# Token tiles ahead of the modulation's weights, and the second half of an output projection prepared during the first

## The chip, the cores and the metric

One Trainium2 chip, and of it one core. A core has five engines with instruction streams of their own: TensorE (PE; its weight loads are PEld in the profile), VectorE (DVE), ScalarE (ACT), GpSimd (POOL) and SyncE (SP), and 16 DMA engines that move data between the large memory and the on-chip buffers. In this kernel nearly all transfers are issued by SP, in the order of its stream. The metric is the time of one execution in microseconds on the device, as the median over runs.

## The reference

A trunk of two layers over 1024 tokens of width 1024. Each layer normalises the rows, modulates them with a shift and a scale that come from a conditioning vector c, mixes tokens, projects back and adds the gated result. The first layer's mixer is a gated DeltaNet with 16 value heads of 128, the second a softmax attention with a forget gate.

```python
cond = jax.nn.silu(c)
for i in range(DEPTH):                                  # DEPTH = 2
    mod = cond @ ada_w[i] + ada_b[i]                    # 1024 -> 3 * 1024
    shift, scale, gate = jnp.split(mod[:, None, :], 3, axis=-1)
    h = rmsnorm(x, norm_w[i]) * (1 + scale) + shift
    y = gdn_mixer(h, ...) if i == 0 else fox_mixer(h, ...)
    x = x + gate * y
return rmsnorm(x, final_norm_w)

def gdn_mixer(h, w_in, conv_w, A_log, dt_bias, norm_w, w_out):
    qkv, z, b, a = split(h @ w_in)                      # 1024 -> 6176
    ...                                                 # conv, SiLU, l2 norms, gated delta rule
    o = rmsnorm(o, norm_w) * jax.nn.silu(z)
    return o.reshape(B, S, 2048) @ w_out                # 2048 -> 1024
```

All is float32. The change touches two places of the first layer: the norm and modulation at the very start, and the product with `w_out`.

## The kernel before

Products of full accuracy are made from three fast ones: each operand is split into a rounded part `hi` and a rest `lo`, and `mm3` adds hi·hi, hi·lo and lo·hi. `split` does this: ACT rounds (a cast), DVE or POOL subtracts.

The order of TensorE's instructions is written out by the program: `Flow` keeps a clock of its own and a list of generators with priorities, and lets each emit work when its wait (a yielded number, or `hold` on a condition) is over; `flow.bank` hands out PSUM banks and `flow.free` returns them. The other engines' streams, SP's among them, are ordered by a scheduler from dependences and program order. Buffers are named tiles with a number of copies: a new use of a copy waits until the last reader of its former content is done.

**The start.** `start_norm` (called by `proj_all`) handles the first 512 tokens in four tiles of 128 x 1024 from `x` (512 KB each; in `vtok` and once in a `d` tile): `norm_tile` takes the sum of squares on ACT, scales on DVE, and transposes on TensorE into the banks `tr`; ACT copies the result out. Then `ada_load(0)` and `ada_load(1)` fetch shift and scale columns of `ada_w`, eight tiles of 512 KB each, into tiles that are idle then (`og`, `zg`, `gb`, `vt` and `d`; several tiles of different tags print as `d`). DVE accumulates the first KPE of them (7, then 5) into one tile, and `ada_sum` adds the others and that one over partitions with matmuls into the bank `su`; the result gives `gcol` and `scol` for four of the eight feature blocks, and `modulate(k)` makes `ht_h` and `ht_l` of each block and multiplies it with a small weight (`wbh`, `wbl`) into the bank `pc`. Only then can the projections run (`mm` banks, weights `whi`, `wlo`).

**The output projection.** `out_proj_a` computes 1024 tokens by 2048 inputs by 1024 columns in two halves of 512 tokens (h=0, 1), each in two pairs of token tiles (tp=0, 2). The gated DeltaNet's output stands in DRAM as `og_d` and `ogl_d` (hi and lo), 16 blocks k of 128 features. For h=0 columns go in two strips of 512, a weight tile (512 KB) holds two k, and the rows of a k come by `out_o` into `ohi` and `olo` (128 KB each, four copies). For h=1 all 1024 columns go at once, a weight tile is one k, four PSUM banks are used (`mm` and, from the next stage, `lg`), and the rows come by `out_pair`, two k at a time, into `yh` and `yl` (256 KB each, four copies). These two tiles and the `lg` banks belong to the second stage's pools, which open only when the DeltaNet's are given back.

Weights pass through `wtile`: a raw tile (three copies, in the space of `ht_h`), then `whi` (three copies) and `wlo` (five). `w_src` and `o_src` list loads not yet begun, `wq` and `oq` hold those begun; `wnext(ahead)` keeps `ahead` k in `wq`, `oload(n)` keeps n in `oq`. `out_list(h)` fills the lists of a half; before, `out_list(1)` is called at the top of h=1, after the wait for the second stage's banks. In the trace's names `ht_h<-in_wa_o_dram` is such a weight load, `tg` (a `wlo` tile) takes the evacuation, and `x_d` and `v` are the finished rows written and read again by the second layer's norm.

Of the kernel before, what the change touches and what calls it, by code (L numbers as in the profile page):

```python
# [15 lines left out]
P = 128  # L16
D = 1024
# [3 lines left out]
HALF = 512  # L21
# [57 lines left out]
SC = 1.0  # L79
OGW = 2000  # L80
OL = 4
Y_NN = 8000
KPE = (7, 5)
KC = 3
# [110 lines left out]
def tile_trunk(  # L195
# [173 lines left out]
    wq, w_src, wcache = [], [], {}  # L369
    oq, o_src = [], []  # L370
# [3 lines left out]
    def half(n=1):  # L374
        for _ in range(min(n, len(later))):
            later.pop(0)()

    def wload():
        half(2)
        if w_src:  # L380
            wq.extend(w_src.pop(0)())
            if not w_src or w_src[0].__name__ == "load_out":
                oload(2)

# [3 lines left out]

    def wnext(ahead):
        half(2)  # L390
        while len(wq) < ahead and w_src:
            wload()
        return wq.pop(0)

    def wtile(n):
# [52 lines left out]
    def out_pair(k, tok):  # L448
        def load():
            w = 2 * P  # L450
            pr = []
            for n, d in (("yh", og_d), ("yl", ogl_d)):
                v = where["py"].tile([P, 2, w], F32R, name=n, tag=n, bufs=4)
                nc.sync.dma_start(v.bitcast(F32), d[k : k + 2, :, tok : tok + w].rearrange("k p t -> p k t"))
                pr.append(v)
            return [(pr[0][:, i], pr[1][:, i]) for i in range(2)]

        return load

    def out_list(h):  # L460
        n = (512, D)[h]
        for tp in range(0, CPH, 2):
            for cs in range(0, D, n):
                w_src.extend(out_w(k, cs, n) for k in range(0, 16, D // n))
                if h:
                    o_src.extend(out_pair(k, h * HALF + tp * P) for k in range(0, 16, 2))
                else:
                    o_src.extend(out_o(k, tp * P) for k in range(16))

    def out_proj_a():  # L470
        gx = xt_([P, 4, D], "ht_h")
        gb0 = gx[:, 0]
        where["raw"] = [gx[:, i] for i in range(1, 4)]
        for h in range(2):
            n = (512, 1024)[h]
            if h:
                yield from hold(lambda: "bank" in where)
                yield OGW
                out_list(1)
            xs = xt_([P, CPH, D], "ht_l")  # L480
            for tp in range(0, CPH, 2):
                for cs in range(0, D, n):
                    acc = None
                    for k in range(16):
                        wh, wl = wnext((5, 3)[h])
                        oload((OL, 7)[h])
                        hi, lo = oq.pop(0)
                        if acc is None:
                            acc = []
                            for b in range(2 + 2 * h):  # L490
                                acc.append((yield from (acc_bank if b < 2 else where["bank"])()))
                        if (tp, cs, k) == (0, 0, 2):
                            if h == 0:
                                nc.sync.dma_start(gb0, gate_d[0:1, :].broadcast_to([P, D]))
                            for t in range(CPH):
                                r0 = (h * CPH + t) * P
                                nc.sync.dma_start(xs[:, t], x[r0 : r0 + P, :])
                        for t in range(2):
                            o = slice(t * P, (t + 1) * P)
                            for c in range(n // 512):  # L500
                                wc = slice(c * 512, c * 512 + 512)
                                mm3(acc[2 * c + t], hi[:, o], lo[:, o], wh[:, wc], wl[:, wc], k == 0, k == 15)
                            if h:
                                yield 0
                        if not h:
                            yield 0
                    for t in range(2):
                        for c in range(n // 512):
                            c0 = cs + c * 512
                            tg = xt_([P, D], "wlo", 5)[:, 0:512]  # L510
                            nc.vector.tensor_tensor(tg, acc[2 * c + t], gb0[:, c0 : c0 + 512], op=ALU.mult)
                            flow.free(acc[2 * c + t], R_OA + 600 * (2 * c + t))
                            xv = xs[:, tp + t, c0 : c0 + 512]
                            nc.gpsimd.tensor_tensor(xv, xv, tg, op=ALU.add)
                for t in range(tp, tp + 2):
                    nc.sync.dma_start(x1_d[h * CPH + t], xs[:, t])
                    if h:
                        where["n2read"](h * CPH + t, xs[:, t])
                    xdone[h * CPH + t] = flow.t

    with ExitStack() as sa:
# [36 lines left out]
        def start_norm():  # L558
# [58 lines left out]
                nc.vector.tensor_tensor(scol[0][:, cs], ps[:, 0:4], bcol[:, 0, cs], op=ALU.add)  # L617
                flow.free(ps, R_AD)

            pc = yield from pst("tr", 2)  # L620

            def modulate(k):
                xk = xsT[k]
                sc, sh = gcol[0][:, k : k + 1], scol[0][:, k : k + 1]
# [6 lines left out]
                mm3(pc[0:32], wbh[:, k], wbl[:, k], ht_h[:, k], ht_l[:, k], k == 0, k == KT - 1)  # L631

            ws = ada_load(0)
            split(wbh, wbl, wba, lo_eng=nc.vector)
            yield from ada_sum(0, ws)
            for k in range(4):
# [1298 lines left out]
```

## Time and profile before

| | |
|---|---|
| median of 3 runs | 1959.63 us (1958.54 to 1962.46) |
| the profiled execution | 1963.85 us, span 1962.1 us |
| mean granted TensorE clock | 0.976 |
| busy: PE, PEld, DVE, ACT, POOL | 93%, 78%, 68%, 53%, 19% of the span |
| moved by DMA | 307 MB, mean 157 GB/s |

A row of the timeline gives start, duration, engine, line, operation, the tile written, the tiles read, and the count of instructions that were put together; in brackets stands how long the engine stood idle before it and what ended that. Line numbers are those of the kernel before. A row of the chain gives start, duration and what the end of the program hung on at that time. A row of stretches gives the stretch, its length, the busy time (and count) of PE, PEld, DVE, ACT and POOL, the granted clock, the share of the DMA engines and GB/s. A matmul's own duration (0.39 us) is longer than the step from one to the next (0.23), since they overlap.

### The profile page before, as it was taken

To read this page: it belongs to the slowest core of one execution; us is meant where nothing else is said; L and a number is where in the kernel's file an instruction comes from. 1 tells how busy PE (TensorE), PEld (TensorE's weight loads), DVE (VectorE), ACT (ScalarE), POOL (GpSimd) and SP (SyncE) were. 2 spreads that over 40 slices of the span, in tenths; PEclk is the share of its full clock that TensorE was granted. 3 is DMA by queue.
4 is the path that set the end of the run, shared out by engine and by line. 5 is a ranking of instruction groups with operands and counts; after the bars stand their busy time and mean duration, and the time that the engine had idled before them with its cause. 6 is when DMAs were issued, how large, how long until landed. Compare 5 with 4: busy or idle time off the path is not lost.

```text
span 1962.1 us, 35871 instructions
## 1 busy us (share of the span) xinstructions
PE 1825.4 (93%) x12888; PEld 1522.8 (78%) x12888; DVE 1326.6 (68%) x3323; ACT 1031.5 (53%) x2674; POOL 365.8 (19%) x402
## 2 busy tenths in 40 slices
PE   5989999989999999999898599999999999999798
PEld 4767787777787777888776478788988988889676
DVE  5586988788887678776655386365666656656764
ACT  4465666655654555555444353365556556655631
POOL 1010111111110100110001144223133132231322
PEclk9889999999999999999999799999999999999899
DMA  7475757677666556454589893011011111111422
GB/s 267 162 239 183 237 192 241 217 227 235 225 185 196 175 169 199 149 171 133 184 275 321 320 308 134 18 60 65 18 60 49 44 60 39 49 54 65 157 88 94
DMA packets 224922, 307.16 MB, mean 157 GB/s; under 512 B 100397, under 2 KB 136877, under 8 KB 224745
## 3 DMA queue, kind: packets, MB, share of 16 engines
q1 hardware_dynamic: 223736, 304.65, 47.8%
q8 instruction: 101, 1.65, 0.4%
q14 instruction: 77, 0.62, 0.1%
q10 hardware_dynamic: 1008, 0.23, 0.1%
HBM read 223.15 MB, written 81.67 MB: 155 GB/s over the span
## 4 chain that ended last, share of the span: by engine, by line
PE 68%; DMA 12%; DVE 12%; ACT 4%; issue 2%; SPq 1%; POOL 1%; ACTq 0%; DVEq 0%; POOLq 0%
PE mm L136 42%; PE lg L136 6%; PE su L136 4%; PE pt L140 4%; PE oT L136 3%; PE tr L140 3%; PE ch L136 3%; DMA nx<-in_ada_w_dram 2%; PE co L136 2%; DVE wlo L339 2%; DMA ht_h<-in_wa_o_dram 1%; DMA ohi<-og_d 1%; DMA rmat<-rb 1%; DVE cv_y L824 1%; ACT whi L336 1%
## 5 line engine op out<-in xcount | busy, mean ns | idle before, releaser
L136 PE MATMUL mm<-ht_h,whi 128*128 128x512 f32 x768 | 342.7, 446 | 0.5 <-DVE nh L312 0.5
L136 PE MATMUL mm<-ht_h,wlo 128*128 128x512 f32 x768 | 305.6, 398 | 0.0
L136 PE MATMUL mm<-ht_l,whi 128*128 128x512 f32 x768 | 304.9, 397 | 0.2 <-POOL ht_l L339 0.2
L136 PE MATMUL mm<-whi,h_h 128*128 128x384 f32 x512 | 186.5, 364 | 0.9 <-DVE kn L1524 0.9
L136 PEld LDWEIGHTS mm<-ht_h,wlo 128*128 128x128 f32 x768 | 146.5, 191 | 33.6
L136 PE MATMUL mm<-whi,h_l 128*128 128x384 f32 x512 | 172.5, 337 | 0.0
L136 PE MATMUL mm<-wlo,h_h 128*128 128x384 f32 x512 | 172.4, 337 | 0.0
L136 PEld LDWEIGHTS mm<-ht_h,whi 128*128 128x128 f32 x768 | 147.6, 192 | 28.7 <-issue 2.1
L1675 DVE TENSOR_TENSOR ptl<-pt,pth 128x512 fp32r<-128x512 f32 x192 | 106.3, 555 | 93.1 <-ACT pth L1674 91.4
L136 PEld LDWEIGHTS mm<-ht_l,whi 128*128 128x128 f32 x768 | 147.9, 193 | 24.4 <-POOL ht_l L339 0.6
L1674 ACT CAST pth<-pt 128x512 fp32r<-128x512 f32 x192 | 91.2, 476 | 141.2 <-PE pt L140 140.5
L824 DVE SCALAR_TENSOR_TENSOR cv_y<-cv_t,conv_h,cv_y 128x512 f32<-128x512 f32 x192 | 143.3, 746 | 17.6 <-ACT cv_y L816 15.3
L339 DVE TENSOR_TENSOR wlo<-ht_h,whi 128x512 fp32r<-128x512 f32 x124 | 93.2, 792 | 56.0 <-ACT whi L336 46.7
L1639 ACT ACTIVATE lg<-lg,mx 128x896 f32<-128x896 f32 (+7 forms) x128 | 99.5, 777 | 54.3 <-DVE mx L1631 48.5
L1518 POOL TENSOR_TENSOR rs<-ss,mhalf 128x4 f32<-128x4 f32 x64 | 64.5, 1007 | 331.1 <-DVE ss L1516 328.4
L336 ACT CAST whi<-ht_h 128x512 fp32r<-128x512 f32 x124 | 70.7, 618 | 90.5 <-PE mm L136 38.1
L136 PE MATMUL mm<-h_h,whi 128*128 128x512 f32 x240 | 100.5, 419 | 0.7 <-DVE wlo L1774 0.3
L136 PEld LDWEIGHTS mm<-whi,h_h 128*128 128x128 f32 x512 | 97.5, 190 | 3.5 <-ACT v L1520 1.2
L140 PE MATMUL pt<-ident,lg 128*128 128x128 f32 (+1 forms) x584 | 96.1, 274 | 3.5 <-ACT lg L1639 3.5
L136 PEld LDWEIGHTS mm<-wlo,h_h 128*128 128x128 f32 x512 | 96.9, 189 | 2.0
L136 PEld LDWEIGHTS mm<-whi,h_l 128*128 128x128 f32 x512 | 96.2, 188 | 0.0
L136 PE MATMUL mm<-h_h,wlo 128*128 128x512 f32 x240 | 94.9, 395 | 0.0
(384 smaller groups left out, 4486.5 us busy)
## 6 DMA issues: line engine op xcount, KB each, us to landing
ht_h<-in_wa_o_dram SPq DMA_DIRECT2D x62, 512.0 KB, 5.3
wc<-whi SPq DMA_DIRECT2D x45, 512.0 KB, 4.2
wc<-wlo SPq DMA_DIRECT2D x45, 512.0 KB, 4.2
wlo<-wc SPq DMA_DIRECT2D x45, 512.0 KB, 4.8
whi<-wc SPq DMA_DIRECT2D x45, 512.0 KB, 3.6
wlo<-in_wa_c_dram SPq DMA_DIRECT2D x35, 512.0 KB, 4.7
nx<-in_ada_w_dram SPq DMA_DIRECT2D x64, 256.0 KB, 3.5
wraw<-in_wb_dram SPq DMA_DIRECT2D x56, 256.0 KB, 2.7
```

The source lines that it names most:

```text
L136: self.nc.tensor.matmul(out, lhsT, rhs, start=start, stop=stop)
L140: self.nc.tensor.transpose(out, src, ident)
L336: nc.scalar.copy(hi, src)
L339: (lo_eng or nc.gpsimd).tensor_tensor(lo, src, hi.bitcast(F32), op=ALU.subtract)
L824: nc.vector.scalar_tensor_tensor(y, raw[:, j : j + HALF], w[:, j : j + 1], y, op0=ALU.mult, op1=ALU.add)
L1518: nc.gpsimd.tensor_tensor(rs, ss, mhalf[:, 0:4], op=ALU.pow)
L1639: nc.scalar.activation(lg, lg, AF.Exp, scale=-1.0, bias=mx[:, hh : hh + 1], accum_out=sums[:, tt : tt + 1],)
L1674: nc.scalar.copy(ph_[:, cs], pp[:, cs])
L1675: nc.vector.tensor_tensor(pl_[:, cs], pp[:, cs], ph_[:, cs].bitcast(F32), op=ALU.subtract)
```

## The change

At the start `ada_load(0)` is called before the bank `pc` is taken rather than after it; the token loads keep their place in the program, ahead of both. In the output projection, `out_list(1)` is called during the first half (last strip, k=8) rather than at the top of the second; the first OX=4 blocks k of the second half's first pair use `out_o` (tiles `ohi`, `olo`) in place of `out_pair`; and `wid`, `wno` number the weight tiles in `wq`, so that no more than three of them are in hand at a time.

```diff
+OX = 4
...
+    wid, wno = [], [0]
+
     def wload():
         half(2)
-        if w_src:
-            wq.extend(w_src.pop(0)())
+        if w_src and len(set(wid)) < 3:
+            ws = w_src.pop(0)()
+            wno[0] += 1
+            wid.extend([wno[0]] * len(ws))
+            wq.extend(ws)
             if not w_src or w_src[0].__name__ == "load_out":
                 oload(2)
...
     def wnext(ahead):
         half(2)
-        while len(wq) < ahead and w_src:
+        while len(wq) < ahead and w_src and len(set(wid)) < 3:
             wload()
+        wid.pop(0)
         return wq.pop(0)
...
                 if h:
-                    o_src.extend(out_pair(k, h * HALF + tp * P) for k in range(0, 16, 2))
+                    k0 = 0 if tp else OX
+                    o_src.extend(out_o(k, h * HALF + tp * P) for k in range(k0))
+                    o_src.extend(out_pair(k, h * HALF + tp * P) for k in range(k0, 16, 2))
...
                 yield OGW
-                out_list(1)
...
                         wh, wl = wnext((5, 3)[h])
+                        if not h and (tp, cs, k) == (2, D - n, 8):
+                            out_list(1)
                         oload((OL, 7)[h])
...
-            pc = yield from pst("tr", 2)
-
...
             ws = ada_load(0)
+            pc = yield from pst("tr", 2)
             split(wbh, wbl, wba, lo_eng=nc.vector)
```

The scheduler orders the streams anew. On SP, at the very start, before:

```order
L563 DMA vtok<-in_x_dram 128x1024
L588 DMA og<-in_ada_w_dram 128x2x512
L588 DMA zg<-in_ada_w_dram 128x2x512
L588 DMA d_285<-in_ada_w_dram 128x2x512
L588 DMA og<-in_ada_w_dram 128x2x512
L588 DMA zg<-in_ada_w_dram 128x2x512
L588 DMA gb<-in_ada_w_dram 128x2x512
L588 DMA vt<-in_ada_w_dram 128x2x512
L588 DMA d_300<-in_ada_w_dram 128x2x512
L563 DMA vtok<-in_x_dram 128x1024 x2
L563 DMA d_240<-in_x_dram 128x1024
L414 DMA wlo<-in_wa_c_dram 128x1024
```

and at the same place in the change:

```order
L573 DMA vtok<-in_x_dram 128x1024 x3
L573 DMA d_240<-in_x_dram 128x1024
L598 DMA og<-in_ada_w_dram 128x2x512
L598 DMA zg<-in_ada_w_dram 128x2x512
L598 DMA d_284<-in_ada_w_dram 128x2x512
L598 DMA og<-in_ada_w_dram 128x2x512
L598 DMA zg<-in_ada_w_dram 128x2x512
L598 DMA gb<-in_ada_w_dram 128x2x512
L598 DMA vt<-in_ada_w_dram 128x2x512
L598 DMA d_299<-in_ada_w_dram 128x2x512
L421 DMA wlo<-in_wa_c_dram 128x1024
```

Three of the four token tiles moved from behind the first eight weight tiles to ahead of them. On DVE, around the first `gcol`, before:

```order
L596 SCALAR_TENSOR_TENSOR d_348<-d_355,cond,d_348 128x1024
L596 SCALAR_TENSOR_TENSOR d_348<-og,cond,d_348 128x1024
L596 SCALAR_TENSOR_TENSOR d_348<-zg,cond,d_348 128x1024
L613 TENSOR_TENSOR gcol_88<-su,bcol 128x4
L617 TENSOR_TENSOR scol_90<-su,bcol 128x4
L614 SCALAR_TENSOR_TENSOR gcol_88<-gcol_88,norm_c 128x4
L629 TENSOR_SCALAR k<-k,gcol_88,scol_90 128x512
L630 TENSOR_TENSOR ht_l<-k,ht_h 128x512
L629 TENSOR_SCALAR k<-k,gcol_88,scol_90 128x512
L630 TENSOR_TENSOR ht_l<-k,ht_h 128x512 x2
L339 TENSOR_TENSOR wlo<-wlo,whi 128x512 x2
L630 TENSOR_TENSOR ht_l<-q,ht_h 128x512
```

and in the change (`d_348` is the accumulation of the modulation's second half):

```order
L606 SCALAR_TENSOR_TENSOR d_348<-d_355,cond,d_348 128x1024
L623 TENSOR_TENSOR gcol_88<-su,bcol 128x4
L627 TENSOR_TENSOR scol_90<-su,bcol 128x4
L624 SCALAR_TENSOR_TENSOR gcol_88<-gcol_88,norm_c 128x4
L606 SCALAR_TENSOR_TENSOR d_348<-og,cond,d_348 128x1024
L637 TENSOR_SCALAR k<-k,gcol_88,scol_90 128x512
L606 SCALAR_TENSOR_TENSOR d_348<-zg,cond,d_348 128x1024
L638 TENSOR_TENSOR ht_l<-k,ht_h 128x512
L637 TENSOR_SCALAR k<-k,gcol_88,scol_90 128x512
L638 TENSOR_TENSOR ht_l<-k,ht_h 128x512 x2
L638 TENSOR_TENSOR ht_l<-q,ht_h 128x512
L340 TENSOR_TENSOR wlo<-wlo,whi 128x512 x4
```

Two accumulations moved behind `gcol`, and the splits of a weight tile behind the fourth `ht_l`. On SP, at the end of the first half of the output projection, from the last transfers of DeltaNet's output on, before:

```order
L1133 DMA og_d<-ogh 128x512
L1133 DMA ogl_d<-ogl 128x512
L1133 DMA og_d<-ogh 128x512
L516 DMA x_d<-ht_l 128x1024
L426 DMA ht_h<-in_wa_o_dram 128x1024
L1133 DMA ogl_d<-ogl 128x512
L516 DMA x_d<-ht_l 128x1024
L426 DMA ht_h<-in_wa_o_dram 128x1024 x2
L1363 DMA v<-x_d 128x1024
L342 DMA kn<-in_wb_dram 128x512
```

and in the change:

```order
L1142 DMA og_d<-ogh 128x512
L1142 DMA ogl_d<-ogl 128x512
L450 DMA ohi<-og_d 128x256
L450 DMA olo<-ogl_d 128x256
L450 DMA ohi<-og_d 128x256
L433 DMA ht_h<-in_wa_o_dram 128x1024
L450 DMA olo<-ogl_d 128x256
L450 DMA ohi<-og_d 128x256
L450 DMA olo<-ogl_d 128x256
L433 DMA ht_h<-in_wa_o_dram 128x1024
L450 DMA ohi<-og_d 128x256
L1142 DMA og_d<-ogh 128x512
```

The rows of the second half's k=0 to 3 are new there (the last `olo` of them follows two rows on), and two weight loads moved up. A few rows on, SP's stream up to the first `yh` and `yl`, before:

```order
L1363 DMA v<-x_d 128x1024
L342 DMA kn<-in_wb_dram 128x512
L1363 DMA v<-x_d 128x1024
L342 DMA kn<-in_wb_dram 128x512
L1363 DMA v<-x_d 128x1024
L1418 DMA qk_c<-in_qkn_dram 128x2
L454 DMA yh<-og_d 128x2x256
L1421 DMA fb<-in_f_bias_dram 128x16
L454 DMA yl<-ogl_d 128x2x256
```

and in the change, where the first `yh` holds k=4 and 5:

```order
L433 DMA ht_h<-in_wa_o_dram 128x1024
L1372 DMA v<-x_d 128x1024
L343 DMA kn<-in_wb_dram 128x512
L1372 DMA v<-x_d 128x1024
L433 DMA ht_h<-in_wa_o_dram 128x1024
L343 DMA kn<-in_wb_dram 128x512
L1372 DMA v<-x_d 128x1024
L1427 DMA qk_c<-in_qkn_dram 128x2
L1430 DMA fb<-in_f_bias_dram 128x16
L461 DMA yh<-og_d 128x2x256
L461 DMA yl<-ogl_d 128x2x256
```

Weight loads moved in among the norm's tiles, ahead of the first `yh`. The order of TensorE's instructions is the same in both; only the tiles that 48 matmuls read have other names.

## The prediction

> **What bounds the kernel now.** First the page: TensorE is busy 93% of the span, so only a stretch in which it stands still, or waits for its data, can give time.
>
> ```profile
> PE 1825.4 (93%) x12888; PEld 1522.8 (78%) x12888; DVE 1326.6 (68%) x3323; ACT 1031.5 (53%) x2674; POOL 365.8 (19%) x402
> ```
>
> The profiled execution took 1963.85 us, 1.75 of it outside its span of 1962.1, and lies 4.2 us above the median of the runs (1959.63). I sum against it and carry the difference to the median. The edit touches two such stretches, and I read each by itself: the chain that ended last, then SP's queue, then the transfer rate. The first is the start, before any projection runs:
>
> ```profile
> 10.90 8.12 DMA vtok<-in_x_dram
> ...
> 25.59 1.97 PE tr L140 x8
> 27.57 1.12 PE tr L140 x4
> 28.69 6.63 PE su L136 x32
> ...
> 35.34 0.16 DVE gcol L613
> ...
> 35.80 2.93 ACT ht_h L625 x4
> ```
>
> The chain goes over the token tiles: the sums `su` stand behind the transposes `tr` on TensorE, and the transposes wait for tiles that were asked for behind eight weight tiles:
>
> ```profile
> 10.39 0.47 SPq L588 DMA_DIRECT2D d<-in_ada_w_dram  x1
> 10.90 1.40 SPq L563 DMA_DIRECT2D vtok<-in_x_dram  x2
> 12.35 0.65 SPq L563 DMA_DIRECT2D d<-in_x_dram  x1
> ```
>
> The next two fences have the rate (share of the transfer engines 1.02, 379 GB/s: full), and the last accumulation of the first half of the modulation on DVE, the use of the last token tile, and the sums; "x16" are eight matmuls in two passes each.
>
> ```profile
> 3.00:35.00 32.00, 14.42 (x64) 12.85 (x64) 19.99 (x28) 12.69 (x46) 6.15 (x15) 1.00 1.02 379
> ```
>
> ```profile
> 18.62 1.28 DVE L596 SCALAR_TENSOR_TENSOR d<-vt,cond,d 128x1024 f32<-128x1024 f32 x1
> ...
> 21.65 1.06 ACT L318 ACTIVATE nx<-d 128x1024 f32<-128x1024 f32 x1
> ...
> 28.48 3.41 PE L136 MATMUL su<-cond,d 128*128 128x1 f32 x16
> 31.75 3.55 PE L136 MATMUL su<-ones,d 128*128 128x1 f32 x16
> ...
> 43.59 1.84 PE L136 MATMUL su<-cond,gb 128*128 128x1 f32 x16
> ```
>
> The second stretch is the step from the first to the second half of the output projection: the longest single wait of TensorE there, its matmuls around it, and the chain's two transfers.
>
> ```profile
> PE mm L136 <- DMA yh<-og_d: 19.3, 1, 19.3
> ```
>
> ```profile
> 1089.36 0.39 PE L136 MATMUL mm<-whi,olo 128*128 128x512 f32 x1
> 1109.00 0.76 PE L136 MATMUL mm<-whi,yh 128*128 128x512 f32 x1 [19.25 <-DMA yh<-og_d]
> ...
> 1114.20 0.63 PE L136 MATMUL lg<-whi,yl 128*128 128x512 f32 x1
> 1114.62 0.63 PE L136 MATMUL mm<-whi,yh 128*128 128x512 f32 x1
> ...
> 1115.40 0.40 PE L136 MATMUL mm<-whi,yl 128*128 128x512 f32 x1
> 1115.63 0.40 PE L136 MATMUL lg<-whi,yh 128*128 128x512 f32 x1
> ...
> 1123.33 0.40 PE L136 MATMUL mm<-whi,yh 128*128 128x512 f32 x1
> ...
> 1126.13 1.04 PE L140 MATMUL pt<-ident,wraw 128*128 128x128 f32 x8
> 1126.92 0.48 PE L136 MATMUL mm<-whi,yh 128*128 128x512 f32 x1
> ```
>
> ```profile
> 1095.20 6.07 DMA ht_h<-in_wa_o_dram
> ...
> 1101.29 7.58 DMA yh<-og_d
> ```
>
> TensorE waits for rows (`yh`), not for weights. After the wait it steps by 0.43 us (1114.20 to 1114.62) until about 1115.2, then by 0.23 (1115.40 to 1115.63): the stop costs some 3 us more. From k=4 (1123.33) on nothing disturbs it for long.
>
> **The change at the start.** Same transfers, another order. A token tile and a weight tile are both 512 KB, and the queue is full in both orders, so the last weight of the first half becomes the twelfth large tile, as the last token tile was: it is there at about 21.65. The token work (squares, transposes, copies) is now done before that. DVE takes 1.28 per weight, about the pace of arrival (0.52 MB at 379 GB/s: 1.38), so it ends a microsecond after. Then the sums, 3.41 + 3.55, and gcol at 21.65 + 7.0 = 28.65 instead of 35.34: 6.7 us earlier. Against it stands DVE's new order: two accumulations of the second half (1.28 each) now stand between gcol and the first `ht_l`, while two splits of weight tiles that stood ahead of the last of the four `ht_l` go behind it. By the rows that is between 1.6 us lost and 1 us won; I take 0.4 lost, since TensorE needs all four. Start: 6.3 us. The later weights of the modulation come no later than before (the same bytes ahead of them), and they are needed only about 8 us after gcol, as the 43.59 row shows against 35.34. The small transfers on ACT's queue and the projection weight behind the block keep their place: nothing. All that follows hangs on h, so I let the whole program move with it. One unknown: TensorE's pace. The sums took 3.5 us per 16 at 28 and 31 us and 1.84 at 43.59; if the earlier start misses that fast spell, `gb` and `vt` lose 1.7 each. Bounds for the start: 6.7 - 1.6 - 3.4 = 1.7, and 6.7 + 1 = 7.7.
>
> **The change at the halves.** Three edits, one place. The list of the second half is filled eight k earlier; rows k=0..3 go to the `ohi`/`olo` buffers, which are free as the first half runs out, not to `yh`/`yl`; a limit of three tiles in hand keeps the earlier list from running over `whi`. The weights were early already: three of the second half's wide tiles (128x1024) stand in SP's queue ahead of the first half's last rows in both orders, their casts ran as buffers came free, and only the subtraction waited, behind the last evacuation.
>
> ```profile
> 1086.64 1.14 ACT L336 CAST whi<-ht_h 128x512 fp32r<-128x512 f32 x2 [2.64 <-PE mm L136]
> ...
> 1089.79 1.14 ACT L336 CAST whi<-ht_h 128x512 fp32r<-128x512 f32 x2 [0.50 <-PE mm L136]
> ```
>
> ```profile
> 1089.11 1.37 DVE L511 TENSOR_TENSOR wlo<-mm,ht_h 128x512 f32<-128x512 f32 x2 [1.32 <-PE mm L136]
> 1090.40 2.97 DVE L339 TENSOR_TENSOR wlo<-ht_h,whi 128x512 fp32r<-128x512 f32 x2
> ```
>
> So the rows decide. Their loads join SP's queue at about 1085, when the transfer engines fall idle:
>
> ```profile
> 1087.00:1089.00 2.00, 2.00 (x10) 1.61 (x10) 0.75 (x1) 1.11 (x3) 0.00 (x0) 1.00 0.18 66
> 1095.00:1100.00 5.00, 0.00 (x0) 0.00 (x0) 1.38 (x3) 0.00 (x0) 0.00 (x0) 0.50 0.99 348
> 1111.00:1113.00 2.00, 2.00 (x6) 1.52 (x6) 0.00 (x0) 0.00 (x0) 0.00 (x0) 0.50 1.02 408
> ```
>
> ```profile
> DMA to landing us min/median/max: 3.4/4.5/5.1
> ```
>
> That is `ohi` in the last 40 us of the first half: 1085.3 + 4.5 = 1089.8. k=0 then starts when the first evacuation has freed its bank, 1089.11 + 0.69, at about 1090 instead of 1109. Four k of 12 matmuls at 0.233 are 11.2 us, so rows are short again at 1101.2. The pair k=4,5 still goes by `yh`. In SP's new order two more weight loads (k=6 and 7) stand ahead of it, and the second needs a raw buffer free, which asks that TensorE has used weight 1 (1090 + 5.6 = 1095.6), then a cast (1.14) and a subtraction (1.29): 1098. Five issues and the wait for older transfers follow (from kn to yh it took 2.5 before): about 1101.5 to 1102, hardly later than the 1101.29 of before. Landing takes 7.1 to 7.6:
>
> ```profile
> ht_h<-in_wa_o_dram SPq DMA_DIRECT2D x6, 512.0 KB, 5.4
> ...
> yh<-og_d SPq DMA_DIRECT2D x6, 256.0 KB, 7.1
> yl<-ogl_d SPq DMA_DIRECT2D x6, 256.0 KB, 8.4
> ```
>
> So k=4 runs at 1109: 14.3 us before its 1123.33, after a new stop of 7.8 us. It starts slow again (12 x 0.43 = 5.1 instead of 2.8), the transposes behind it too, and after k=5 k=6 could start at 1118. But the next `yl` (k=6,7) stands behind four token tiles, two weights and three `yh` now: 4.2 MB with itself, at 400 GB/s (of 348 and 408 above, nearer to the later) 10.5 us after 1109.5. So k=6 at 1120.0 instead of 1129.7 (1126.92 + 2.8): 9.7 us won, of 19 that the wait held. From there SP waits for buffers that TensorE frees, so pace and gain stay. Bounds: 4 (the transfer rate, full from 1095 on, decides and eats the rest) and 21.9 (19.0 and the 2.9 of the slow start, no second stop).
>
> What a slow start costs is told by the row below: after 2.62 us of rest eight passes take 1.97, where they took 1.04 at 1126.13.
>
> ```profile
> 1173.73 1.97 PE L140 MATMUL pt<-ident,wraw 128*128 128x128 f32 x8 [2.62 <-DVE wraw L1344]
> ```
>
> The Trainium skill, TensorE: Matmul & The Clock Gate (Part 1: The HAM clock gate), has the clock halved after an idle window of about 3.4 us; by that the new stop of 7.8 us costs a slow start, as the row says, and 2.62 us would not always, where the row has it. The Trainium skill, DMA: Bandwidth & Descriptors (Specifications), speaks against this change: memory gives a core about 358 GB/s, so earlier asking brings nothing where that is used up; the 4.2 MB would then take 11.7 us and the gain at the halves be 8.5. The window at 1111 has 408, and the measurement decides.
>
> Sum: 6.3 + 9.7 = 16.0: the profiled execution from 1963.85 to about 1947.9, the median from 1959.63 to 1943.6; I say 1943.5.
>
> **The rivals.**
> - No second stop: the `yh` of k=4 lands by 1101. For it: engines idle from 1087 to 1094; against: its place behind weight 7. 6.3 + 21.9: 1931.
> - Transfers set the pace of the second half, and the halves give 3 to 4: 1950. For it: 0.99 and 1.02 above. Against: TensorE ran on from 1115 without a long wait.
> - The start gives nothing (weights later by what the rows are earlier, or slow sums), the halves stay: 9.7, so 1950.
> - The change does nothing that counts: both waits only move. The weights of the second half were early already, so that part of its words is true of the kernel before. 1959.
> - Slower: SP's queue works in order, and the loads of weights 6 and 7 now wait in it for TensorE, ahead of norm2's tiles, `yh` and all else. If k=0 starts late, at S, `yh` is issued at S + 11.7 and k=4 runs at S + 19. That passes 1123.33 at S = 1104, and with the start's 6.3 and the 3.9 of the bound it is slower from S = 1114 on, 29 us after the issue of the rows; the longest landing is 5.1. At S = 1118 k=4 runs at 1137, 13.7 late, less 6.3: 1967.
>
> **How the numbers follow.** 0.2% of the time, 3.9 us, is about what a measurement of this kernel can tell from no change. Chances: forecast 0.55, no second stop 0.08, transfers 0.15, start without gain 0.12, nothing 0.06, slower 0.04. The range reaches from 1936 (half of the way to the case without a stop) to 1953 (the two cases near 1950 and their spread) and leaves out 0.18. Faster 0.90, same 0.06, slower 0.04. The forecast's own range is 1938 to 1949.
>
> **What would show it.** Right at the start: four x loads first in SP's queue, gcol near 28.7, the first projection matmul 6 us before 63.87. Right at the halves: TensorE idle under 2 us between the last `olo` matmul and the first with `ohi` in a `lg` bank; 48 such matmuls; then a wait of 5 to 9 us for `yh`, and perhaps one of up to 3 for `yl`. Wrong: a wait for `ohi`, `whi` or a bank in place of the old one; a start whose sums come later than 31; or new waits between k=6 and the end of the half, which would give the gain back.

## The result

The changed kernel takes 1948.59 us (median of 20 runs, 1937.06 to 1956.45) against 1959.05 us for the kernel before (20 runs, 1953.43 to 1966.38). The ratio is 0.9943 with a 95% interval of 0.9930 to 0.9956: 11.2 us won, between 8.6 and 13.7 (the two medians differ by 10.5). Predicted were 16 us and 1943.5 us. So the direction held, and the gain is about 5 us smaller than its sum. The start did what the sum had it do; at the halves the waits came where the prediction placed them, but what limits the gain there is, by the experiments, what its second rival said: the transfer rate. One execution of the kernel without token tiles (below), 3544 us where the others took 1939 to 1950, is not in its ratio.

The profiled execution of the changed kernel took 1945.78 us, 18.1 less than that of the kernel before. That pair overstates the gain, as shown below.

**The start** came out as the sum had it. First SP's queue in the changed kernel (start, duration, line, transfer): the four token tiles are first, the weights behind.

```profile
1.24 1.37 SPq L573 DMA_DIRECT2D vtok<-in_x_dram  x3
2.89 0.33 SPq L573 DMA_DIRECT2D d<-in_x_dram  x1
5.21 0.38 SPq L598 DMA_DIRECT2D og<-in_ada_w_dram  x1
```

The timeline of TensorE and DVE (line numbers are up to ten higher than before): the first sums, gcol, and the first matmul of the projection.

```profile
22.30 3.58 PE L137 MATMUL su<-cond,d 128*128 128x1 f32 x16 [3.95 <-DMA d<-in_ada_w_dram]
25.74 3.55 PE L137 MATMUL su<-ones,d 128*128 128x1 f32 x16
...
29.51 0.16 DVE L623 TENSOR_TENSOR gcol<-su,bcol 128x4 f32<-128x4 f32 x1
...
58.30 0.80 PE L137 MATMUL mm<-ht_h,whi 128*128 128x512 f32 x1
```

The sums now wait for the weights alone. gcol is at 29.51 instead of 35.34, 5.8 us earlier, and the first projection matmul at 58.30 instead of 63.87, 5.6 us earlier; 6.3 was the term.

**The halves.** TensorE in the changed kernel: the last matmul of the first half, k=0 of the second with `ohi`/`olo`, its first matmul in an `lg` bank, the last of k=3, and k=4 with `yh`.

```profile
1077.84 0.40 PE L137 MATMUL mm<-whi,olo 128*128 128x512 f32 x1
1078.58 0.47 PE L137 MATMUL mm<-whi,ohi 128*128 128x512 f32 x1 [0.35 <-DMA ohi<-og_d]
...
1079.35 0.40 PE L137 MATMUL lg<-whi,ohi 128*128 128x512 f32 x1
...
1089.35 0.39 PE L137 MATMUL lg<-whi,olo 128*128 128x512 f32 x1
1099.33 0.76 PE L137 MATMUL mm<-whi,yh 128*128 128x512 f32 x1 [9.59 <-DMA yh<-og_d]
...
1110.13 0.50 PE L137 MATMUL mm<-whi,yl 128*128 128x512 f32 x1 [1.52 <-DMA yl<-ogl_d]
```

The wait of 19.3 us is gone. k=0 starts 0.7 us after the first half's last matmul, four k run without a stop, and then TensorE waits 9.6 us for the row tiles of k=4, and 1.5 us for `yl` of k=6. So over half of the old wait has come back at the place that the prediction named; the 9.6 us are just above the 5 to 9 that it gave as its sign.

**What the profiled pair says, in parts.** I cut the span at three rows that every kernel has: the first matmul of the projection; the matmul twenty before the second half's first; and the first matmul of the projection that follows the second half. The last two stand in the kernel before and in the changed one at

```profile
1085.47 0.40 PE L136 MATMUL mm<-whi,olo 128*128 128x512 f32 x1
...
1211.40 0.33 PE L136 MATMUL mm<-whi,h_h 128*128 128x384 f32 x1
```

```profile
1072.79 0.39 PE L137 MATMUL mm<-whi,olo 128*128 128x512 f32 x1
...
1192.27 0.33 PE L137 MATMUL mm<-whi,h_h 128*128 128x384 f32 x1
```

Below, the part between these two rows is called the stretch: 125.9 us before, 119.5 after. The span became 18.3 us shorter: 5.6 at the start, 7.1 in the middle part, 6.4 in the stretch, and 0.8 lost behind it. The middle part runs the same code in both kernels but for its last 15 us. At one place in it, near 160 us, TensorE waits for `nh` (made by DVE) in the kernel before, 1.2 and 0.5 us, and then runs at half clock for some 7 us. At the same matmuls the changed kernel waits 0.5 us alone and keeps its clock. These are the waits of the kernel before, then of the changed one (in us, their number, the longest one):

```profile
PE tr L136 <- DVE nh L700: 1.7, 2, 1.2
```

```profile
PE tr L137 <- DVE nh L709: 0.7, 2, 0.5
```

It is not the new start that does this: a kernel with the old start (the halves alone, below) doesn't wait for `nh` there and keeps its clock too. First the window of the kernel before, then that kernel's; the last numbers of a window are granted clock, DMA share and GB/s.

```profile
163.10:169.70 6.60, 6.52 (x27) 5.47 (x28) 2.84 (x5) 1.22 (x2) 0.22 (x2) 0.50 0.33 120
```

```profile
156.00:166.00 10.00, 9.32 (x67) 7.51 (x66) 7.04 (x15) 4.20 (x9) 1.30 (x4) 1.00 0.66 238
```

In nine of the 14 traces of this study TensorE waits 0.6 to 1.4 us at that matmul, and in all nine half clock follows, for 6.8 us in seven and 3.4 in two. Of the five without this wait, four keep the full clock there. The Trainium skill, TensorE: Matmul & The Clock Gate (Part 1: The HAM clock gate), says that the activity window is free-running and doesn't start with the kernel. That about equal waits, 1.24 us in the kernel before and 1.28 in the sixth experiment, are followed by 6.8 and 3.4 us of half clock agrees with it.

Over the whole middle part the clock doesn't explain the pair. These are the kernel before, the changed one, and the start alone (below):

```profile
63.87:1085.47 1021.60, 963.34 (x8165) 781.98 (x8165) 760.79 (x1987) 563.90 (x1651) 112.91 (x171) 0.98 0.66 209
```

```profile
58.30:1072.79 1014.49, 966.31 (x8166) 785.07 (x8165) 760.71 (x1989) 564.10 (x1651) 114.59 (x171) 0.98 0.66 210
```

```profile
58.34:1086.17 1027.83, 976.63 (x8165) 791.93 (x8165) 761.60 (x1987) 565.38 (x1651) 113.82 (x171) 0.97 0.65 208
```

The changed kernel's TensorE is busy 3 us longer than that of before, and not busy for 48.2 us instead of 58.3: it gained its 7.1 us there by shorter waits. The start alone was slow there by a longer busy time, at a lower clock. Over the 14 traces the middle part took 1013.5 to 1027.8 us. This scatter alone is as large as the gain, and no single pair of profiles can size the change; the stretch, the start and the medians can.

### The profile page after: what moved, and what is told of

It reads as the page before. It is cut to its first block, busy times and chain, and to the rows that moved or that the text cites. A ratio compares the mean times of both kernels' runs of the same rounds, so it can differ in the third digit from the quotient of the medians.

```text
span 1943.8 us, 35877 instructions
## 1 busy us (share of the span) xinstructions
PE 1828.4 (94%) x12888; PEld 1524.4 (78%) x12888; DVE 1328.3 (68%) x3323; ACT 1033.3 (53%) x2674; POOL 367.0 (19%) x402
## 4 chain that ended last, share of the span: by engine, by line
PE 62%; DMA 14%; DVE 13%; ACT 4%; issue 3%; POOL 1%; SPq 1%; ACTq 0%; DVEq 0%; POOLq 0%
PE mm L137 39%; PE lg L137 5%; PE su L137 4%; PE pt L141 3%; PE oT L137 3%; DMA nx<-in_ada_w_dram 3%; PE tr L141 3%; PE ch L137 2%; DVE wlo L340 2%; PE co L137 2%; DVE cv_y L833 2%; DMA ohi<-og_d 2%; DMA rmat<-rb 1%; DMA wraw<-in_wb_dram 1%; ACT whi L337 1%
```

## The experiments

All were timed beside the kernel before. Each has a trace, and the table is worked out from the starts of the three rows named above (us).

| kernel | first projection matmul | from there to the stretch | stretch | rest | ratio to before (95%) |
|---|---|---|---|---|---|
| before | 63.87 | 1021.6 | 125.9 | 750.7 | |
| changed | 58.30 | 1014.5 | 119.5 | 751.5 | 0.9943 (0.9930–0.9956) |
| changed, again | 60.68 | 1018.1 | 116.7 | 751.1 | 0.9954 (0.9936–0.9972) |
| start alone | 58.34 | 1027.8 | 123.2 | 751.9 | 0.9966 (0.9944–0.9987) |
| halves alone | 63.66 | 1014.8 | 118.7 | 750.3 | 0.9960 (0.9942–0.9978) |
| rows early, weights not | 57.07 | 1015.7 | 126.5 | 747.8 | 0.9983 (0.9961–1.0006) |
| weights early, rows not | 57.77 | 1017.0 | 124.8 | 747.8 | 0.9958 (0.9943–0.9973) |
| OX = 8 | 57.22 | 1021.0 | 124.3 | 750.2 | 0.9963 (0.9944–0.9982) |
| rows of k=4–7 first | 58.46 | 1019.2 | 120.4 | 750.9 | 0.9960 (0.9942–0.9977) |
| rows of k=4–15 first | 57.87 | 1013.5 | 119.9 | 747.7 | 0.9954 (0.9935–0.9973) |
| needed first | 57.96 | 1017.3 | 118.0 | 752.4 | 0.9933 (0.9910–0.9956) |
| and norm2 later | 57.45 | 1018.3 | 119.4 | 749.5 | 0.9935 (0.9912–0.9957) |
| and no token tiles | 57.63 | 1015.8 | 113.5 | 755.5 | 0.9920 (0.9888–0.9952) |
| norm2 later, kn later | 57.51 | 1015.5 | 122.0 | 750.1 | 0.9942 (0.9918–0.9966) |

**1. The start alone**, in the kernel before:

```
-            pc = yield from pst("tr", 2)
...
             ws = ada_load(0)
+            pc = yield from pst("tr", 2)
```

> The start's part alone, in the kernel before: the first weights of the modulation are asked for before the transpose bank, nothing is changed at the halves. By my theory it gives 6 us (0.997 of the time before): the first projection matmul 5.6 us before 63.9, the stop of 19 us at the halves as it was, k=0 of the second half near 1103. Rival A: the 4.0 us that the changed kernel's trace gained between 149 and 171 us belong to the start as well, then 10 us (0.995). Rival B: the start gives nothing at the end and the halves give all of the 11 us: 0 (1.000).

0.9966: 6.7 us (2.5 to 11.0), as my theory. The 12 traces with this start have their first projection matmul at 58.0 us in the mean, the two without it at 63.8: 5.8 us. Rival B falls, since the interval excludes no gain. Rival A is within the interval, but the trace speaks against it: with this start, too, TensorE waits for `nh` near 153 us, 0.7 us, and half clock follows for 6.8. In its trace the stop at the halves is still there:

```profile
PE mm L136 <- DMA yh<-og_d: 19.5, 1, 19.5
```

The profiled span of this kernel, 1961.3, is hardly below that of before (1962.1). Its middle part took 1027.8 us; between 460 and 780 us the granted clock was 0.96 in it, and 0.98 in the halves-alone kernel, and 2642 matmuls were done against 2722 (the first "x", behind TensorE's busy time):

```profile
460.00:780.00 320.00, 305.34 (x2642) 249.78 (x2641) 245.32 (x651) 174.14 (x531) 35.34 (x49) 0.96 0.62 190
```

```profile
460.00:780.00 320.00, 307.55 (x2722) 251.84 (x2712) 249.08 (x665) 177.47 (x541) 35.50 (x49) 0.98 0.62 196
```

**2. The halves alone**: the changed kernel with the transpose bank taken ahead of `ada_load(0)` again.

> The halves' three edits alone, without the start. By my theory 6.5 us (0.9967): counted by the number of the matmul, the changed kernel's lead over the kernel before was 12.7 us ahead of the halves and 19.1 after them; k=0 starts 17 to 18 us earlier, k=4 stops 9 to 10 us for yh, yl of k=6 or 7 stops 1 to 2 more. Rival A: 9.7 us, the size in the prediction (0.995). Rival B: the lead at the halves is given back before the end of the program, 0 to 2 us (0.999 to 1.000).

0.9960: 7.8 us (4.3 to 11.4); the time can't tell 6.5 from 9.7. The trace does: a stop of 8.3 us for `yh`, 1.9 for `yl`, stretch 118.7. The two kernels with the old step at the halves have stretches of 125.9 and 123.2, the three with the new one (changed, again, halves alone) 119.5, 116.7 and 118.7. Means 124.5 and 118.3: the halves give 6.2 us, not 9.7. Start and halves sum to 12.0 by the traces, and 11.2 was measured; by time alone they sum to 6.7 + 7.8 = 14.5, each good to about 4 us.

**3. Rows early, weights not**, and **4. weights early, rows not** (OX = 0); `out_list` is told which of the two lists to fill:

```
 if not h and (tp, cs, k) == (2, D - n, 8):
-    out_list(1)
+    out_list(1, "o")      # 3: rows;  4: "w", weights
...
     yield OGW
+    out_list(1, "w")      # 3: weights;  4: "o", rows
```

> The changed kernel with the second half's weights entered at the old place (at the start of the second half) and only its rows entered early, OX = 4. By my theory the rows decide: k=0 starts without a stop of over 2 us, then the stop for yh of k=4 is 9 to 12 us (two token tiles stand ahead of it now instead of two weights), the whole time 9 to 11 us below the kernel before (0.9945 to 0.9955), as the changed kernel. Rival: the early weights matter as well, then a stop of 5 us or more for a weight's cast or subtraction at k=0 to 3 and the gain is that of the start alone, 6 us (0.997).

> The counterpart of the run with rows alone: the second half's weights are entered early, its rows at the old place and all by yh/yl (OX = 0), the start as in the changed kernel. If the rows alone open k=0: the stop at k=0 is 17 to 19 us as in the kernel before, and the time is that of the start alone, 6 us below the kernel before (0.997). If it is the early weights that carry what the halves gave (the run with rows alone lost its lead of 31 us by waits after k=4): the stop is the same, but the stretch after it runs faster, and the time is 9 to 12 us below the kernel before (0.994 to 0.9955).

My theory that the rows decide falls. With rows alone the stretch is 126.5, with weights alone 124.8, where neither gives 124.5: each part alone is worth nothing there, and only both together give 6.2. With rows alone, k=0 does start early (1077.59), but then TensorE waits for what the rows were moved past, more and longer than in the changed kernel:

```profile
PE mm L137 <- DMA yh<-og_d: 11.1, 1, 11.1
PE mm L137 <- DVE wlo L340: 2.9, 4, 1.2
...
PE lg L137 <- DVE wlo L340: 1.4, 2, 0.7
```

With weights alone it waits for the first `yh` as before, 15.9 us. By time, 3 agrees with the start alone or less (0.9983); 4, at 0.9958, is between my two numbers, and its interval takes in the changed kernel. For 4 only one trace says that the stretch was not faster. The transfer rate goes with the stretches: in the 60 us from the first row of the stretch on, 307 GB/s were moved before, 317 with the start alone, 319 with rows alone and 332 with weights alone, but 347, 349 and 352 in the three traces with both. Between the means of the old step and the new, 312 and 349, lie 2.2 MB, at 400 GB/s 5.6 us.

**5. OX = 8.**

> The changed kernel with OX = 8: the rows of k=4 to 7 too go by ohi/olo, which in SP's queue puts them ahead of norm2's three tiles. By my theory the second stop is a matter of place in a queue whose transfers run at full rate: k=4 to 7 run without a stop, k=8 is ready at 1101 and its yh and yl land at 1102 to 1105, a stop of 1 to 4 us in place of 9.6 + 1.5, so 6 to 9 us less than the changed kernel (0.990 to 0.9915 of the kernel before). Rival A: the transfers set the pace, the stop only moves to k=8 and stays 8 to 11 us long: no gain over the changed kernel (0.994 to 0.995). Rival B: SP waits for the four ohi buffers that TensorE frees and the weights behind them come late: a stop for whi or wlo and slower than the changed kernel (over 0.996).

Neither the stop at k=8 nor a gain: k=4 and 5 run, with one wait of 3.5 us for norm2's tile between them, and k=6 waits 10.5 us for `ohi`. The scheduler put the `ohi` of k=6 and 7 behind the four token tiles and the `yh` of k=8 to 15. Stretch 124.3, no gain at the halves; it is rival A's outcome with the stop at another k, and of B's waits for weights there is none.

**6. The rows of k=4 to 7 first**, and **7. of k=4 to 15**:

```
+with tc.high_priority(150 if tok == HALF and k < 8 else 0):     # 7: k < 16
     nc.sync.dma_start(v.bitcast(F32), d[k : k + 2, ...])
```

> The changed kernel, with the yh and yl of k=4 to 7 put ahead of norm2's tiles in SP's queue (a higher priority for the scheduler, nothing else). By my theory the second stop is place in a full queue: yh of k=4 is issued at 1085 to 1087 instead of 1093.4, lands at 1091 to 1094 instead of 1099.3, the stop shrinks from 9.6 to 1 to 4 us, the wait for yl goes, and the whole is 6 to 9 us below the changed kernel (0.990 to 0.9915 of the kernel before). Rival (transfers set the pace of the whole stretch, which run at 400 GB/s from 1084 to 1114 in the changed kernel): the bytes put behind come back as waits for weights or for rows of k=8 and later, and no more than 2 us is won over the changed kernel (0.9935 to 0.995).

> As the run with the rows of k=4 to 7 first, but for the rows of k=4 to 15: 3 MB of rows stand ahead of norm2's tiles and of the weights 6 and later. By my theory (place in the queue) the stop at k=4 is 1 to 5 us, as there, and a wait of 2 to 5 us for weight 6 comes in, since six row transfers stand ahead of it: 3 to 7 us below the changed kernel (0.991 to 0.993 of the kernel before). Rival (transfers set the pace): the same time as the run with k=4 to 7 first, and both as the changed kernel (0.994).

The stop for `yh` is gone altogether in both, and nothing is won: stretches 120.4 and 119.9 against 118.3. The waits of 6 on TensorE:

```profile
PE pt L142 <- DVE wraw L1355: 4.9, 3, 2.7
PE mm L138 <- DVE wlo L341: 3.3, 1, 3.3
PE mm L138 <- ACT whi L338: 3.0, 1, 3.0
```

What stood ahead of the rows before, norm2's tiles (`wraw`) and weights (`whi`), is now late instead. This is the rival's case, that the transfers set the pace. The 3.3 us for `wlo` are less clear: they end at 1135.19, behind the full part of the stretch (share 0.87 from 1130 to 1135), and DVE, which makes `wlo`, is on a tile of norm2 from 1131.98 to 1134.5.

**8. What is needed first**: 6, and norm2's three tiles and the second half's token tiles at a lower priority. **9. And norm2 later**: its first tile 14 us later in the planner.

```
+with tc.high_priority(-150 if h else 0):       # 8, 9
     nc.sync.dma_start(xs[:, t], x[r0 : r0 + P, :])
...
+with tc.high_priority(-100):                   # 8, 9
     nc.sync.dma_start(xt, x1_d[t])
...
-yield 2500
+yield 2500 if t else 16500                     # 9
```

> The run with the rows of k=4 to 7 first, and beside it norm2's three tiles and the second half's four token tiles get a lower priority, so that in SP's queue the rows and weights of the output projection stand ahead of them. TensorE's order is unchanged, norm2's transposes included. Measured by the stretch from 5 us before the end of the first half to the first matmul of the projection that follows (124.5 us in the kernel before and with the start alone, 118.3 as the mean of three traces with the change at the halves, 120 with the rows first). By my theory, that the bytes which stand ahead of what TensorE asks for next make the waits: no stop over 2 us for yh, whi or wlo, but the transposes, 57 matmuls into the second half, wait 4 to 9 us for norm2's tiles, which are now loaded late; stretch 110 to 116, whole time 2 to 8 us below the changed kernel (0.990 to 0.994 of the kernel before). Rival (the transfers as a whole set the pace, in whatever order): 118 to 120, and the whole as the changed kernel (0.9945).

> The run before, and norm2's first tile is also taken up 14 us later by the kernel's own planner, which puts its transposes 123 matmuls into the second half instead of 57. Nothing that TensorE needs in the first 28 us of the second half stands behind anything else now. By my theory the stretch (124.5 before, 118.3 changed) falls to 101 to 106, with less than 6 us of idle time on TensorE in it instead of 15, and the whole is 11 to 17 us below the changed kernel (0.986 to 0.989 of the kernel before). Rival (the transfers set the pace): rows, weights and tiles ask for more than 400 GB/s in any order, the stretch stays at 115 to 120 and the whole at 0.993 to 0.995.

The rival holds in both: 118.0 and 119.4. In 8 the wait has gone over to the transposes of norm2's tiles. In 9 those wait hardly at all, and the weights come late instead (first 8, then 9):

```profile
PE pt L142 <- DVE wraw L1356: 10.4, 2, 8.2
PE mm L138 <- ACT whi L338: 2.8, 1, 2.8
```

```profile
PE mm L138 <- ACT whi L338: 6.3, 3, 3.5
PE mm L138 <- DVE wlo L341: 3.1, 3, 2.7
```

The 2.7 us of 9 are not a wait for a transfer. They end at 1132.39, where the engines are no longer full (share 0.42 from 1125 to 1130), and on DVE a tile of norm2 stands ahead of the `wlo`:

```profile
1127.71 4.02 DVE L1356 TENSOR_SCALAR wraw<-v,ln_rs 128x512 f32<-128x512 f32 x2 [0.68 <-POOL ln_rs L1343]
1131.66 3.57 DVE L341 TENSOR_TENSOR wlo<-ht_h,whi 128x512 fp32r<-128x512 f32 x4
```

In both orders, as in the changed kernel, the transfer engines are full for 30 to 40 us (share 1.02 to 1.04, about 390 GB/s; the changed kernel, then 9):

```profile
1080.00:1112.00 32.00, 20.89 (x85) 16.48 (x84) 15.52 (x31) 11.49 (x23) 6.68 (x6) 0.84 1.02 387
```

```profile
1084.00:1124.00 40.00, 33.23 (x131) 25.66 (x130) 16.31 (x32) 16.15 (x32) 5.58 (x5) 0.91 1.04 396
```

**10. No token tiles**: 9 without 2.1 MB of loads; it leaves the second half's tokens out of the residual. **11. kn later**: 9 with 256 KB loads at a lower priority, nothing left out.

```
-with tc.high_priority(-150 if h else 0):       # 10
+if not h:
     nc.sync.dma_start(xs[:, t], x[r0 : r0 + P, :])
...
+with tc.high_priority(-400):                   # 11
     bload(raw[:, k % 2])
```

> The run with norm2 later, without the four loads of token tiles for the second half (2.1 MB less in the stretch; the residual's token tiles of the second half are left out of the sum, an operation of the same size on GpSimd adds the product to itself). If the transfers as a whole set the pace of the stretch, it falls from 119.4 by 2.1 MB at 400 GB/s, 5 us, to 113 to 116, and the waits for the weights' casts near 1118 and 1132 (3.5 and 2.7 us) shrink by as much; the whole time 0.9905 to 0.9925 of the kernel before. If it is not bytes but SP's waits for buffers or the casts themselves, the stretch stays at 118 or more, and the whole at 0.993 to 0.995.

> The run with norm2 later, and the loads of the second mixer's first weights (kn, 256 KB each; four of them stood in the full part of the stretch) get a lower priority, nothing is left out. By the transfers' theory up to 1 MB leaves the full part, 2.6 us: stretch 116 to 118 against 119.4, the whole 0.9915 to 0.9935 of the kernel before; this would be the fastest version. Rival: no change, 119 to 121, since the waits are those of SP for weight buffers.

10 is the only kernel whose stretch falls clearly, from 119.4 to 113.5 in one trace each: 5.9 us for bytes that take 5.2 us at 400 GB/s. In windows of 5 us the engines are full from 1085 to 1120 in 9, and from 1080 to 1110 in 10. The wait of 3.5 us for `whi`, 1117.9 in 9, is gone and one of 0.9 stands shortly behind; the one of 2.7 us, which was DVE's, is now 2.1, less of a drop than expected. The two rows of its stretch, and these two waits:

```profile
1073.44 0.40 PE L138 MATMUL mm<-whi,olo 128*128 128x512 f32 x1
...
1116.05 0.50 PE L138 MATMUL lg<-wlo,yh 128*128 128x512 f32 x1 [0.92 <-DVE wlo L341]
...
1123.33 0.50 PE L138 MATMUL mm<-wlo,yh 128*128 128x512 f32 x1 [2.12 <-DVE wlo L341]
...
1186.90 0.33 PE L138 MATMUL mm<-whi,h_h 128*128 128x384 f32 x1
```

Behind the stretch this kernel took 755.5 us instead of 749.5, with one wait of 3.5 us for ACT in the second mixer; it computes on other values there, and the cause stays open. Its ratio, 0.9920, can't be told from 9's. In 11 the stretch is 122.0: the rival's number, nothing won. Only two of the four small loads left their place, ahead of norm2's tiles; the other two stood behind the token tiles already. So 0.5 MB left it, 1.3 us at 400 GB/s, which one trace can't show; 11 does not support the transfers' theory, and its rival, SP's waits for weight buffers, is not excluded by it.

None of these versions is measurably faster than the changed kernel: 8 and 9 come lowest of those that compute everything, and their intervals take in its 0.9943.

**12. The changed kernel again.**

> The changed kernel once more, unchanged, beside the others on their chip: for the ratio against them and for a second trace. Expected 0.9943 of the kernel before, 0.993 to 0.9956. By my theory the profiled pair's 18.3 us against 11 of the medians is scatter of TensorE's half-clock intervals at places that the edit doesn't touch: in this trace the lead over the trace before at matmul 8300 differs from 12.7 by several us, while the stop for yh (9 to 10 us) and the lead gained between matmul 8320 and 8700 (6 to 7 us) stay. Rival: the 12.7 us are the edit's own and come again.

0.9954. Stretch 116.7, the stop for `yh` 8.9 us; the lead over the trace of before at the mark twenty matmuls ahead of the second half is 6.7 us instead of 12.7, so the theory of scatter holds, though waits make it as well as the clock, as shown above. But in the stretch, too, the lead grew by 9.2 us instead of 6 to 7: one pair of traces is good to about 3 us there, and the 6.2 us above rest on means of two and three.

## Why the prediction was right, and where its sum was off

**The start**: predicted 6.3, measured 5.6 in the pair, 5.8 over all traces, 6.7 (2.5 to 11.0) by time. The last weight came 0.65 us later than in the sum (22.30 against 21.65), the sums took 7.2 instead of 7.0. The 4 us that the profiled pair gained between 149 and 171 us are not the start's but the wait for `nh` and the half clock behind it in the trace before.

**k=0 of the second half**: predicted 19 us earlier by TensorE's own progress. Measured 1109.00 - 1078.58 = 30.4, less the 12.7 that the trace led by already: 17.7. The last rows of the first half came late by 1.2 us, since the new loads stand among them.

**The second stop** is the term that was mis-sized: 7.8 predicted, 9.6 measured (8.9 again, 8.3 with the halves alone). The working had weight 7 issued at 1098 and `yh` of k=4 at 1101.5 to 1102, so 3.5 to 4 us and five issues later. SP's queue in the changed kernel shows what it took:

```profile
1085.02 0.44 SPq L1372 DMA_DIRECT2D v<-x_d  x1
1086.18 0.33 SPq L343 DMA_DIRECT2D kn<-in_wb_dram  x1
1086.55 0.46 SPq L1372 DMA_DIRECT2D v<-x_d  x1
1087.14 0.41 SPq L433 DMA_DIRECT2D ht_h<-in_wa_o_dram  x1
1088.35 0.33 SPq L343 DMA_DIRECT2D kn<-in_wb_dram  x1
1089.60 0.33 SPq L1372 DMA_DIRECT2D v<-x_d  x1
1090.83 0.33 SPq L1427 DMA_DIRECT2D qk_c<-in_qkn_dram  x1
1092.07 0.33 SPq L1430 DMA_DIRECT2D fb<-in_f_bias_dram  x1
1093.35 0.38 SPq L461 DMA_DIRECT2D yh<-og_d  x1
```

From the weight at 1087.14 on each issue comes about 1.24 us after the one ahead, 6.2 us from the weight to `yh`. The chain of SP's waits names the releaser: `yh` waits for the `v` that was issued at 1085.02, eight transfers ahead of it in the queue, and so does each of the others for the eighth ahead of its own.

```profile
SPq L461 <- DMA v<-x_d: 0.9, 1, 0.9
...
SPq L1427 <- DMA x_d<-ht_l: 0.9, 1, 0.9
```

So SP goes on here at the pace of the transfers. The prediction took 2.5 us, from `kn` to `yh`, from the trace of before. There `yh` waited for the eighth ahead as well, the weight issued at 1095.20 in the chain that the prediction shows. But the issues right ahead of `yh` were not held up: what stood eight ahead of them had been issued by 1094.41, while the engines had room (share 0.53 from 1090 to 1095). That weight 7 itself came 8.6 us after k=0, where the sum had 8.0, is luck: the sum had it wait for a raw buffer that TensorE frees, and in the trace it follows the `v` of 1086.55 without such a wait. Landing then took 6.0 us instead of the 7.1 to 7.6 taken, and k=4 ran 1123.3 - 1099.3 - 12.7 = 11.3 us earlier, not 14.3.

**The restart at half clock** (0.43 us per matmul until 1103.7) cost 2 us, as said, though the transposes behind it ran at full clock. **`yl`**: 1.5 us, within the 3 allowed. After it the lead won at the halves was 7.3 instead of 9.7, and 6.4 at the end of the stretch.

**The rivals.** Of the five it is the second, transfers at their limit, that the forecast should have given more weight: it said 3 to 4 us for the halves, the forecast 9.7, the measurement 6.2. The trace of before had the number for it, in the eight us when TensorE has begun to wait and the transfer engines are two thirds empty:

```profile
1087.00:1095.00 8.00, 2.75 (x12) 1.91 (x11) 6.64 (x8) 2.54 (x5) 2.94 (x2) 0.99 0.38 132
1095.00:1125.00 30.00, 15.99 (x56) 12.36 (x57) 7.42 (x15) 8.08 (x16) 5.58 (x5) 0.66 1.00 364
```

With a share of 0.38, 5.0 of those 8 us were free; behind them the engines are full for 30 us. If the stretch is bound by its bytes, filling that hole is worth 5.0 us, and its measured gain is 6.2. The prediction read these windows, but spent them on one late `yl`, and followed the rows of one k where it should have followed the sum of the bytes. The prediction also set the Trainium skill's 358 GB/s (DMA: Bandwidth & Descriptors, Specifications) against 400. The changed kernel moves 387 over 32 us and 396 has been seen over 40, so the measurement is above that figure. That there is a ceiling, as the Trainium skill has it, this case shows too, at about 400; experiments 6 to 9 show that another order of asking doesn't get past it.

The evidence is 10 (bytes taken away, the full part of the stretch is 5 us shorter and a wait goes) and 6 to 9 (four other orders, stretch 118.0 to 120.4). It holds for the full part of the stretch; behind it DVE's work makes waits too, 2.7 us in 9. 10 took four places in SP's queue away along with the bytes, and no run separates the two; but the engines are full while SP waits, which speaks for the bytes. Why an early list of rows alone, or of weights alone, moves fewer bytes is not followed row by row; that each alone has no gain in the stretch is one trace each.

That the median, 1948.59, is inside the forecast's own range, 1938 to 1949, is in part luck: the start's term came true, and the halves gave less than the forecast and more than the rival, for the rival's reason.

## What to carry to other kernels

Ahead of moving a load forward, read how full the transfer engines are in the stretch where the wait stands and in the one behind it: the idle share ahead of the wait, times its length, is an estimate of what earlier asking can give, here 5.0 us of a wait of 19.3, where 6.2 were measured. Where the engines were full behind it, another order only moved the wait (from `yh` to norm2's transposes, to the weights), and what helped was fewer bytes; moving 0.5 MB to a later time showed no gain. For a change below one per cent, cut the span at rows that all kernels have and look at the part that was changed; the spans of one pair of profiles here differed by 18.3 us, where the medians differ by 10.5.

## What the runs showed of the hardware that I had not expected

A small load costs its place, not its size: `qk_c` and `fb`, 1 and 8 KB, each held SP's queue for about 1.24 us, as a tile of 512 KB did, since each waited for the transfer eight places ahead. The transfer engines were full meanwhile (share 1.03, 412 GB/s from 1089 to 1094), so the place cost the loads behind it time, not the engines. Whether the eight are a limit of the chip or of how the program numbers its waits no run here shows.

The half clock also comes after waits of about a microsecond: at one matmul near 160 us (0.50 for the 6.6 us from 163.1) it followed in all nine traces in which TensorE waits 0.6 to 1.4 us there, and not in four of the five in which it doesn't. Waits and half clock together make the middle part 1013.5 to 1027.8 us long. The executions of the changed kernel differ by 1% (1937.06 to 1956.45 us); that such places make all of this is not shown.
